# A 3x3 convolution with residual: first image in one load, residuals and stores two pairs at a time

## The chip, the cores and the metric

One core of one Trainium2 chip. Times are device microseconds of a whole execution; the lower the better. The traced span, from the kernel's first instruction to its last, is shorter than that time.

## The reference

```python
# x, residual: 16 x 64 x 64 x 64 float32; weight: 64 x 64 x 3 x 3
x_pad = np.pad(x, ((0, 0), (0, 0), (1, 1), (1, 1)))
for b, co, ci, kh, kw in all_of_them:
    output[b, co] += weight[co, ci, kh, kw] * x_pad[b, ci, kh:kh+64, kw:kw+64]
return output + residual
```

The inputs x and residual are 16.8 MB each, and so is the output. With 0.15 MB of weights, 50.48 MB cross the HBM interface, whatever the kernel does.

## The kernel before

Two images (a "pair", 2 MB) fill 128 partitions. ScalarE (ACT) casts an image to bf16, TensorE convolves it into PSUM, and VectorE (DVE) adds the residual in place in SBUF, from where it is stored. SyncE (SP) issues all the DMA but one. The parts that matter:

```python
sem = lambda name: tc.alloc_semaphore(name)
s_x = [sem(f"s_x{i}") for i in range(NXR)]
s_r = [sem(f"s_r{p}") for p in range(NPAIR)]          # one for each residual pair
# ... (20 in all)

for p in range(NPAIR):                                # SyncE
    if p >= NXR:
        nc.sync.wait_ge(s_half, 2 * (p - NXR) + 3)
    if p == 0:
        to_the_front(load_x(p, cols=slice(0, NPIX // 2)))   # before the opening barrier
        nc.sync.dma_start(out=wraw[:, :], in_=w_rows[:, :]).then_inc(s_w, 16)
    else:
        load_x(p)
    load_ro(p)
for p in range(NEARLY):                               # NEARLY = 6
    nc.sync.wait_ge(s_add, 2 * p + 3)
    store(p).then_inc(s_out, 16)
# ...
to_the_front(load_x(0, nc.scalar, slice(NPIX // 2, NPIX)))  # ACT: the image's other half
# ...
for n in range(B):                                    # VectorE
    p, im = divmod(n, 2)
    if im == 0:
        nc.vector.wait_ge(s_r[p], 16)
    # ... two adds; the first waits for the convolution
# ...
for p in range(NEARLY, NPAIR):                        # the last two stores
    store(p)
with tc.tile_critical(sync_engine=mybir.EngineType.Pool, no_gpsimd_drain=True):
    nc.gpsimd.wait_ge(s_out, 16 * NEARLY)             # GpSimd's closing wait
```

The last two stores carry no semaphore in the source. The built program gives each one of its own, and has GpSimd wait for the first of them and SyncE for both.

## Time and profile before

| | before |
|---|---|
| time | 122.9 us (122.8 to 123.06, 3 runs) |
| traced span | 121.17 us in a run of 123.0 us |
| TensorE, VectorE, ACT busy | 72%, 63%, 52% of the span |
| bytes at the full rate | 50.48 MB / 433 GB/s = 116.6 us |

Of the page of before: the span, the head of the chain that ended last, and the table of DMA issues (how many, KB each, us from issue to landing).

```profile
span 121.2 us, 736 instructions
PE 71%; DVEq 2%; DVE 2%; issue 0%
...
ro<-in_residual_dram SPq DMA_DIRECT2D x8, 2048.0 KB, 21.9
out_dram<-ro SPq DMA_DIRECT2D x8, 2048.0 KB, 28.2
xr<-in_x_dram SPq DMA_DIRECT2D x7, 2048.0 KB, 17.5
xr<-in_x_dram SPq DMA_DIRECT2D x1, 1024.0 KB, 7.0
xr<-in_x_dram ACTq DMA_DIRECT2D x1, 1024.0 KB, 7.6
wraw<-in_weight_dram SPq DMA_DIRECT2D x1, 144.0 KB, 6.9
```

The chain names PE, but 2 MB need only 4.86 us at the full rate, so a landing after 22 or 28 us means a queue of four or five transfers ahead of it: the engines are never without work. The prediction shows the slices that confirm it.

### The profile page before, as it was taken

How to read it: one execution, taken by the hardware profiler on the slowest of the kernel's cores; microseconds unless marked ns; L12 is line 12 of the kernel's file. 1: busy time of each engine (PE TensorE's matmuls, PEld its weight loads, DVE VectorE, ACT ScalarE, POOL GpSimd, SP SyncE). 2: the span in 40 equal slices, each digit the busy share in tenths (PEclk: the TensorE clock that was granted, in tenths of full speed). 3: DMA queues.
4: the chain of work that ended last, by engine and by line, in shares of the span. 5: the costliest groups of instructions: out<-in, count | busy, mean ns of one | idle time of the engine just before them, and what ended most of it. 6: DMA issues, size and time to landing. Idle time of an engine off the chain costs nothing.

```text
span 121.2 us, 736 instructions
## 1 busy us (share of the span) xinstructions
PE 87.7 (72%) x389; PEld 10.7 (9%) x105; DVE 76.0 (63%) x40; ACT 63.1 (52%) x37; POOL 2.4 (2%) x16
## 2 busy tenths in 40 slices
PE   0033499999999999999999999999999980000000
PEld 0021001101010101010101010101010100000000
DVE  0005300889898898989889898898989889300000
ACT  4049969938966984993993994896000000000000
POOL 5200000000000000000000000000000000000000
PEclk9999999999999999999999999999999999755555
DMA  6999999999999999999999999999999999999993
GB/s 168 427 444 433 433 433 433 433 427 433 433 427 427 433 433 427 427 433 427 433 433 433 433 433 422 433 389 433 433 433 433 422 433 433 433 433 433 427 433 151
DMA packets 3744, 50.48 MB, mean 417 GB/s; under 512 B 416, under 2 KB 544, under 8 KB 544
## 3 DMA queue, kind: packets, MB, share of 16 engines
q1 hardware_dynamic: 3600, 49.43, 96.3%
q10 hardware_dynamic: 144, 1.05, 2.0%
HBM read 33.70 MB, written 16.78 MB: 417 GB/s over the span
## 4 chain that ended last, share of the span: by engine, by line
PE 71%; DVEq 2%; DVE 2%; issue 0%
PE ps L86 53%; PE ps L85 17%; DVEq L129 2%; DVE ro L201 2%
## 5 line engine op out<-in xcount | busy, mean ns | idle before, releaser
L201 DVE TENSOR_TENSOR ro<-ps,ro 64x2048 f32<-64x2048 f32 x32 | 73.2, 2289 | 17.7 <-PE ps L86 17.2
L86 PE MATMUL ps<-xp,wl 128*128 128x504 bf16 (+1 forms) x288 | 80.0, 388 | 0.2
L173 ACT CAST xp<-xr 64x2048 bf16<-64x2048 f32 x16 | 30.3, 1896 | 19.3 <-DMA xr<-in_x_dram 17.1
L85 PE MATMUL ps<-xp,wl 128*128 128x504 bf16 (+1 forms) x92 | 35.8, 389 | 3.4 <-PEq L222 3.4
L177 ACT CAST xp<-xr 64x2048 bf16<-64x2048 f32 x16 | 30.4, 1897 | 0.4
L85 PEld LDWEIGHTS ps<-xp,wl 128*128 128x128 bf16 x96 | 9.5, 99 | 79.1 <-issue 79.1
L189 DVE CAST wl<-ps 32x192 bf16<-32x192 f32 x8 | 2.8, 348 | 10.4 <-PE ps L214 10.3
L214 PE MATMUL ps<-ident,wraw 128*32 128x128 f32 x9 | 2.1, 412 | 8.1 <-DMA wraw<-in_weight_dram 8.1
L214 PEld LDWEIGHTS ps<-ident,wraw 128*32 128x32 f32 x9 | 1.2, 137 | 8.6 <-issue 8.1
L173 ACT ACT_TABLE_LOAD x1 | 1.3, 1283 | 1.1 <-SPq L129 1.1
L182 ACT CAST wl<-ps 32x192 bf16<-32x192 f32 x4 | 1.2, 306 | 0.0
L160 POOL MEMSET xp<- 64x64 bf16 x4 | 0.6, 147 | 0.2
L159 POOL MEMSET xp<- 64x64 bf16 x4 | 0.6, 145 | 0.2
L148 POOL TENSOR_SCALAR_AFFINE_SELECT ident<-ident 128x128 f32<-128x128 f32 x1 | 0.3, 295 | 0.2 <-POOL ident L146 0.2
L162 POOL MEMSET wl<- 64x192 bf16 x1 | 0.3, 253 | 0.1
L161 POOL MEMSET wl<- 64x192 bf16 x1 | 0.3, 252 | 0.1
L146 POOL MEMSET ident<- 128x128 f32 x1 | 0.2, 205 | 0.7 <-SPq L129 0.7
L257 POOL MEMSET const-uint8-127<- 128x1 uint8 x1 | 0.1, 113 | 0.0
L257 POOL MEMSET const-bfloat16-1.0<- 128x1 bf16 x1 | 0.1, 112 | 0.0
L257 POOL MEMSET const-float32-1.0<- 128x1 f32 x1 | 0.1, 109 | 0.0
L257 POOL MEMSET const-float32-0.0<- 128x1 f32 x1 | 0.1, 104 | 0.2 <-issue 0.2
## 6 DMA issues: line engine op xcount, KB each, us to landing
ro<-in_residual_dram SPq DMA_DIRECT2D x8, 2048.0 KB, 21.9
out_dram<-ro SPq DMA_DIRECT2D x8, 2048.0 KB, 28.2
xr<-in_x_dram SPq DMA_DIRECT2D x7, 2048.0 KB, 17.5
xr<-in_x_dram SPq DMA_DIRECT2D x1, 1024.0 KB, 7.0
xr<-in_x_dram ACTq DMA_DIRECT2D x1, 1024.0 KB, 7.6
wraw<-in_weight_dram SPq DMA_DIRECT2D x1, 144.0 KB, 6.9
```

Of the source, the lines that this page charges most:

```text
L85: return e.matmul(out=out_, lhsT=lhsT, rhs=rhs, start=start, stop=stop, skip_group_check=True)
L86: return e.add_instruction(mybir.InstMatmult(name=nc.get_next_instruction_name(), engine=PE, ins=[e.lower_ap(rhs), e.lower_ap(lhsT)], outs ...
L129: with tc.tile_critical(no_gpsimd_drain=True):
L159: nc.gpsimd.memset(t[0:64, 0, :], 0.0).then_inc(s_id, 1)
L160: nc.gpsimd.memset(t[64:128, J, :], 0.0).then_inc(s_id, 1)
L173: i = nc.scalar.copy(out=t[64:128, 0:J, :], in_=x4[hp, :, 0, :])
L177: nc.scalar.copy(out=t[0:64, 1 : J + 1, :], in_=x4[hp, :, 1, :]).then_inc(s_pack, 1)
L182: i = nc.scalar.copy(**weight_block(h, *b))
L189: i = nc.vector.tensor_copy(**weight_block(h, *b))
L201: i = nc.vector.tensor_tensor(out=o4[hp, :, par, :], in0=psj[64 * par : 64 * par + 64, :, :], in1=o4[hp, :, par, :], op=ADD)
L214: i = nc.tensor.transpose(out=tp[0:32, t // 3, 128 * (t % 3) : 128 * (t % 3) + 128], in_=wraw3[:, :, t], identity=ident[:, :])
L257: nc = _bacc.Bacc("TRN2", target_bir_lowering=False, num_devices=1)
```

## The change

Its intent is economy around the bytes: fewer and larger transfers, fewer semaphores, one queue instead of two. The core of the diff (the renaming of s_wt into counts of s_id and the reshaping of `ro` into one tile are cut):

```diff
-    s_r = [sem(f"s_r{p}") for p in range(NPAIR)]
+    s_r = [sem(f"s_r{i}") for i in range(2)]
+    RES = (slice(0, 1), slice(1, 2), slice(2, 4), slice(4, 6), slice(6, 8))
...
+    def load_ro(i):
+        if i >= 2:
+            nc.sync.wait_ge(s_r[i % 2], 16 * (i // 2))
+        nc.sync.dma_start(out=ro[:, RES[i], :], in_=res_bc[:, RES[i], :]).then_inc(s_r[i % 2], 16)
...
-                to_the_front(load_x(p, cols=slice(0, NPIX // 2)))
+                to_the_front(load_x(p))
...
-            load_ro(p)
-        for p in range(NEARLY):
-            nc.sync.wait_ge(s_add, 2 * p + 3)
-            store(p).then_inc(s_out, 16)
+            if p in (0, 1, 3, 5, 7):
+                load_ro((p + 1) // 2)
+        for k in range(NSTORE - 1):
+            nc.sync.wait_ge(s_add, 4 * k + 5)
+            store(k).then_inc(s_out, 16)
...
-        to_the_front(load_x(0, nc.scalar, slice(NPIX // 2, NPIX)))
...
-            if im == 0:
-                nc.vector.wait_ge(s_r[p], 16)
+            if im == 0 and p in first:
+                i = first.index(p)
+                nc.vector.wait_ge(s_r[i % 2], 16 * (i // 2 + 1))
...
-    for p in range(NEARLY, NPAIR):
-        store(p)
+    store(NSTORE - 1)
```

Here `store(k)` moves pairs 2k and 2k+1, 4 MB.

More of the change, by code (lines that the diff above doesn't have):

```diff
@@ L37 @@
     NXP = 4
-    NEARLY = 6
-    res_bc = residual.rearrange("b c h w -> (b c) (h w)")
-    out_bc = out.rearrange("b c h w -> (b c) (h w)")
+    NZERO = 4 + 2 * NXP
+    NSTORE = NPAIR // 2
+    RES = (slice(0, 1), slice(1, 2), slice(2, 4), slice(4, 6), slice(6, 8))
+    res_bc = residual.rearrange("(p b) c h w -> (b c) p (h w)", b=2)
+    out_bc = out.rearrange("(p b) c h w -> (b c) p (h w)", b=2)
     x_bc = x.rearrange("b c h w -> (b c) (h w)")
@@ L48 @@
     ident = pool.tile([128, 128], FP32)
-    ro = [pool.tile([128, NPIX], FP32, name=f"ro{p}") for p in range(NPAIR)]
+    ro = pool.tile([128, NPAIR, NPIX], FP32)
     xr = [nc.alloc_sbuf_tensor(f"xr{i}", [128, NPIX], FP32) for i in range(NXR)]
@@ L59 @@
     s_x = [sem(f"s_x{i}") for i in range(NXR)]
-    s_r = [sem(f"s_r{p}") for p in range(NPAIR)]
+    s_r = [sem(f"s_r{i}") for i in range(2)]
     s_out = sem("s_out")
     s_id = sem("s_id")
-    s_wt = sem("s_wt")
     s_half = sem("s_half")
@@ L68, with load_x, store @@
     s_add = sem("s_add")
-    def load_x(p, engine=nc.sync, cols=slice(0, NPIX)):
-        return engine.dma_start(out=xr[p % NXR][:, cols], in_=x_bc[128 * p : 128 * p + 128, cols]).then_inc(
-            s_x[p % NXR], 16
-        )
-    def load_ro(p):
-        nc.sync.dma_start(out=ro[p][:, :], in_=res_bc[128 * p : 128 * p + 128, :]).then_inc(s_r[p], 16)
-    def store(p):
-        return nc.sync.dma_start(out=out_bc[128 * p : 128 * p + 128, :], in_=ro[p][:, :])
+    def load_x(p):
+        return nc.sync.dma_start(out=xr[p % NXR][:, :], in_=x_bc[128 * p : 128 * p + 128, :]).then_inc(s_x[p % NXR], 16)
+    def load_ro(i):
+        if i >= 2:
+            nc.sync.wait_ge(s_r[i % 2], 16 * (i // 2))
+        nc.sync.dma_start(out=ro[:, RES[i], :], in_=res_bc[:, RES[i], :]).then_inc(s_r[i % 2], 16)
+    def store(k):
+        pairs = slice(2 * k, 2 * k + 2)
+        return nc.sync.dma_start(out=out_bc[:, pairs, :], in_=ro[:, pairs, :])
     def matmul(out_, lhsT, rhs, start, stop, ldweights):
@@ L171 @@
             if im == 0:
-                nc.scalar.wait_ge(s_x[p % NXR], 16 * (p // NXR + 1 + (p % NXR == 0)))
+                nc.scalar.wait_ge(s_x[p % NXR], 16 * (p // NXR + 1))
             i = nc.scalar.copy(out=t[64:128, 0:J, :], in_=x4[hp, :, 0, :])
@@ L178 @@
             if n == 0:
-                nc.scalar.wait_ge(s_wt, 1)
+                nc.scalar.wait_ge(s_id, NZERO + 1)
                 for b in blocks[4:]:
@@ L182 @@
                         i = nc.scalar.copy(**weight_block(h, *b))
-                i.then_inc(s_wt, 1)
-        nc.vector.wait_ge(s_wt, 1)
+                i.then_inc(s_id, 1)
+        nc.vector.wait_ge(s_id, NZERO + 1)
         for k, b in enumerate(blocks[:4]):
@@ L191 @@
                     i.then_inc(s_bank, 2)
-        i.then_inc(s_wt, 1)
+        i.then_inc(s_id, 1)
+        first = [pairs.start for pairs in RES]
         for n in range(B):
@@ L195 @@
             hp = slice(64 * im, 64 * im + 64)
-            o4 = ro[p].rearrange("q (j two w) -> q j two w", two=2, w=W)
+            o4 = ro[:, p, :].rearrange("q (j two w) -> q j two w", two=2, w=W)
             psj = ps[n % 2].rearrange("q c j w -> q (c j) w")
-            if im == 0:
-                nc.vector.wait_ge(s_r[p], 16)
+            if im == 0 and p in first:
+                i = first.index(p)
+                nc.vector.wait_ge(s_r[i % 2], 16 * (i // 2 + 1))
             for par in range(2):
@@ L207 @@
                 i.then_inc(s_add if par == 0 or n == B - 1 else s_bank, 1)
-        nc.tensor.wait_ge(s_id, 4 + 2 * NXP)
+        nc.tensor.wait_ge(s_id, NZERO)
         nc.tensor.wait_ge(s_w, 16)
@@ L216 @@
             )
-        i.then_inc(s_wt, 1)
-        nc.tensor.wait_ge(s_wt, 3)
+        i.then_inc(s_id, 1)
+        nc.tensor.wait_ge(s_id, NZERO + 3)
         with nc.Fori(0, B // NXP, 1, engines=[PE]):
@@ L236 @@
                 m.then_inc(s_conv, 1)
-    for p in range(NEARLY, NPAIR):
-        store(p)
+    store(NSTORE - 1)
     with tc.tile_critical(sync_engine=mybir.EngineType.Pool, no_gpsimd_drain=True):
-        nc.gpsimd.wait_ge(s_out, 16 * NEARLY)
+        nc.gpsimd.wait_ge(s_out, 16 * (NSTORE - 1))
 _INS = ['x', 'weight', 'residual']
```

## The prediction

> **What bounds the kernel now.** I began with the chain of work that ended last, as one should, and here it misleads: it gives PE 71% of the span, but it ends at the last VectorE add (about 104 us) while the span is 121.2 us. So I went on to the slices and the DMA queues.
>
> ```profile
> PE   0033499999999999999999999999999980000000
> DMA  6999999999999999999999999999999999999993
> GB/s 168 427 444 433 433 433 433 433 427 433 433 427 427 433 433 427 427 433 427 433 433 433 433 433 422 433 389 433 433 433 433 422 433 433 433 433 433 427 433 151
> q1 hardware_dynamic: 3600, 49.43, 96.3%
> q10 hardware_dynamic: 144, 1.05, 2.0%
> HBM read 33.70 MB, written 16.78 MB: 417 GB/s over the span
> ```
>
> The 16 DMA engines are at 9 tenths or more in all slices but the first and the last, at 422 to 444 GB/s but for one dip to 389 near 80 us, where loads give way to stores. TensorE is done at slice 34 of 40. The kernel is bound by its bytes: 50.48 MB at 433 GB/s are 116.6 us. Only 4.6 us of the span are something else. Finer windows say where they are (columns: busy time of PE, PEld, DVE, ACT and POOL, then clock, DMA share, GB/s):
>
> ```profile
> 0.00:1.00 1.00, 0.00 (x0) 0.00 (x0) 0.00 (x0) 0.00 (x0) 0.22 (x4) 1.00 0.00 0
> 1.00:2.00 1.00, 0.00 (x0) 0.00 (x0) 0.00 (x0) 0.92 (x1) 0.59 (x3) 1.00 1.06 197
> 2.00:3.00 1.00, 0.00 (x0) 0.00 (x0) 0.00 (x0) 0.36 (x1) 0.73 (x6) 1.00 0.84 311
> 3.00:4.00 1.00, 0.00 (x0) 0.00 (x0) 0.00 (x0) 0.00 (x0) 0.78 (x5) 1.00 1.00 418
> 119.00:119.50 0.50, 0.00 (x0) 0.00 (x0) 0.00 (x0) 0.00 (x0) 0.00 (x0) 0.50 0.39 164
> 119.50:121.20 1.70, 0.00 (x0) 0.00 (x0) 0.00 (x0) 0.00 (x0) 0.00 (x0) 0.50 0.00 0
> ```
>
> Head: nothing flows for 1.0 us, and against 433 GB/s the next two microseconds lose (236 + 122) / 433 = 0.8 us. Tail: the last bytes are in by about 119.6 us; by the trace's semaphore records the last store is reported landed at 120.21 and the closing barriers run to 121.17. Together 1.0 + 0.8 + 1.6 = 3.4 us; the rest is the 80 us dip and the small weight packets. A change that adds and removes no byte can only win there, or lose by letting the queue run dry.
>
> It does not run dry before the end, because SyncE issues far ahead. The last two stores are issued once the last add is done:
>
> ```profile
> 104.42 0.96 SPq L79 DMA_DIRECT2D out_dram<-ro  x2
> SPq L268 <- DMA out_dram<-ro: 14.8, 2, 10.0
> ```
>
> At 104.42 us the store before them is still in the queue; it is reported at 110.50. SyncE then waits 14.8 us for data. The queue would empty only if the last issue slipped by more than about 4.5 us (110.5 minus 0.6 from last byte to report, minus 1.0 from issue to first packet, minus 104.4).
>
> **What the Trainium skill says.** "DMA: Bandwidth & Descriptors", section "Where 436 GB/s comes from", puts the ceiling of 16 engines at 435 GB/s. This trace agrees: 433 in most slices, so bigger transfers cannot raise the rate. The same page, "Issuing engines are not separate DMA queues": issuing from several engines saves only the sequencer's issue time. The trace agrees and is stronger: ACT's half of the first image was issued at 0.13 us, yet its first packet starts at 2.67 us, after 44 packets of SyncE's queue. The second queue bought nothing in the head. "Latency and other measured facts" there warns of tiles whose per-partition row pitch in HBM is 2 MiB or the like (164 GB/s). The changed transfers have a pitch of 16 KiB from partition to partition and 2 MiB only between a partition's two rows, so I do not expect it to apply; no run here shows it yet. "Why a DMA increments its semaphore by 16 and not by 1" warns of two transfers in flight on one semaphore; this is why the change has SyncE wait before it reuses one of the two residual semaphores.
>
> **The change part by part.**
>
> First image whole on SyncE. The 256 packets of 8 KB become 128 of 16 KB. In steady flow 8 KB takes 309 ns and 16 KB 611 ns, so 16 packets per engine at 309 (4.94 us) become 8 at 611 (4.89): -0.05 us. In the ramp the first packet of an engine took 0.5 to 1.3 us instead of 0.31. If that excess (about 0.6 us, then some 0.2 on the second packet) is a latency per packet or a fixed time, it stays whole; if it is lower speed until about 2.5 us in which a larger packet hides a bit more, some comes back. I take -0.15 us as an estimate. SyncE's first issue stays at time 0, and the barrier behind it, which now waits for no ACT issue (ACT joined it 0.1 us after SyncE), delays nothing that has bytes waiting. The image was complete at 7.75 us and the weights at 8.01 us; both stay within some tenths, as the same 2.24 MB pass first, and the compute chain has slack.
>
> Fewer transfers. 26 become 18. Each ends in one semaphore packet per engine, 9 ns in the trace: 8 x 9 ns = -0.07 us. The landings of 2 MB stores are 4.86 us apart, which their 8 packets of 608 ns fill already, so there is no gap between transfers to close.
>
> Residuals two pairs at a time. The order of loads becomes x2, x3, r2+r3, x4, x5, r4+r5, x6, x7, r6+r7. With the landings of before, x3 comes 4.9 us earlier (37.2 to 32.3) and r2 later, with r3, at 42.08 instead of 32.33. VectorE needs it for image 4:
>
> ```profile
> 42.46 4.61 DVE L201 TENSOR_TENSOR ro<-ps,ro 64x2048 f32<-64x2048 f32 x2 [0.58 <-PE ps L86]
> ```
>
> It is just in time, by 0.4 us. Pair 4 lands at 61.6 for an add at 63.2, pair 6 at 81.3 for an add at 84.0. So no wait arises, and one of 1 us would eat into the 4.5 us above without moving the end. SyncE's new waits (first use of a residual semaphore done) were met long before: r1 at 22.6 for an issue near 37, r2+r3 at 42 for one near 55.
>
> Stores two pairs at a time. The first waits for image 4's add (about 45 us, already over when SyncE gets there), the second for image 8's (65.5), the third for image 12's (86.3). The loads alone fill the engines to about 80.6 us, then each store of 4 MB adds 9.7: to 90, 100 and 109.7. Every issue is ahead of its deadline by 13 us or more; the last, at 104.4, by about the 4.5 us of before.
>
> The end. This is the part that the diff does not show. Before, the last two stores had two semaphores, and GpSimd's closing steps waited for the first alone. They ran under the last one: landed 115.36, GpSimd wakes 115.38, branch 115.47, semaphore 115.62, no-op 115.71. Now there is one last store, and the built program has GpSimd wait for it, while SyncE's final wait needs GpSimd's increment behind that no-op. So 115.71 - 115.36 = 0.35 us that lay under a transfer now follow it: +0.35 us. Fewer semaphores to clear: 200 ns for a range of 29 become, if proportional, 145 for 21: -0.05 us. Both kernels declare the same queues, so the 1.8 us between span and measured time (121.2 and 123.0 in the profiled run) should stay.
>
> Sum: -0.05 - 0.15 - 0.07 + 0.35 - 0.05 = +0.03 us, so 122.9.
>
> **Rivals.** (1) The head wins more: one queue of 16 KB packets reaches full rate at once. For it: between 1.0 and 2.67 us only SyncE's packets ran, 44 of 8 KB; the same 44 of 16 KB would be the full rate. Against: the engines were already occupied end to end by single slow packets. It would bring back those 0.8 us in place of my 0.15: 122.3. (2) The late residual stalls VectorE, then the PSUM banks, then the last issue. For it: only 0.4 us of margin at image 4. Against: a stall of even 2 us is under 4.5. It makes 0; with something unforeseen on top, +1. (3) Two rows 2 MiB apart per partition cost HBM rate. For it: the skill's figures for such strides. Against: at any moment the engines walk neighbouring rows as before. One per cent on the 29.4 MB that move so (residual pairs 2 to 7, 12.6 MB, and all stores, 16.8 MB: 68 us) would be +0.7 us, 123.6; a real collapse, several us. (4) The closing chain stays hidden: -0.35 us, 122.6.
>
> **Range and chances.** Head, tail and rate leave some +-0.6 us (the head up to -0.65 by rival 1, the tail -0.35 by rival 4, the rate +0.7 by rival 3, not all at once): 122.3 to 123.5. 2% is 2.46 us. To gain that, the span would have to be 118.7 us, which leaves 2.1 us beside the 116.6 of the bytes, less than the 1.0 before the first packet and the 1.6 after the last: 1%. To lose it needs rival 3 in force: 3%.
>
> **What would show it.** Right: DMA at 433 from slice 2 to 39; q10 gone; the last load-store order as above; VectorE's add of image 4 near 42.5 us; SyncE's last issue near 104; the last landing near 120.0; from landing to end 1.3 us instead of 0.96. Wrong: slices in the middle under 425 GB/s, a first slice near 250 GB/s, an add that waits for a residual by several us, or a DMA gap near 109 us.

## The result, and the profile after

The changed kernel takes 123.48 us (median, 123.28 to 123.73, 6 runs), before 122.9 (122.8 to 123.14, 6 runs); all were fast runs (none is over 1.5% above the fastest of its kernel). The ratio is 1.0044, 95% interval 1.003 to 1.0058. Ratios here are the mean time of one kernel's fast runs over that of the other's of the same rounds, so not quite the ratio of the medians quoted. The change makes the kernel slower by half a microsecond: "same" at 2%, but clear of noise, and at the edge of the predicted range.

The page of the changed kernel, profiled in its fastest run (123.28 us):

```profile
span 121.2 us, 729 instructions
DMA  7999999999999999999999999999999999999992
GB/s 173 427 416 433 433 433 432 433 433 432 433 432 432 433 432 433 433 432 432 422 427 433 432 433 427 432 422 432 432 433 432 432 427 433 432 432 433 432 432 108
q1 hardware_dynamic: 3488, 50.48, 98.1%
HBM read 33.70 MB, written 16.78 MB: 416 GB/s over the span
...
xr<-in_x_dram SPq DMA_DIRECT2D x8, 2048.0 KB, 15.2
out_dram<-ro SPq DMA_DIRECT2D x4, 4096.0 KB, 28.7
ro<-in_residual_dram SPq DMA_DIRECT2D x3, 4096.0 KB, 24.0
ro<-in_residual_dram SPq DMA_DIRECT2D x2, 2048.0 KB, 15.8
wraw<-in_weight_dram SPq DMA_DIRECT2D x1, 144.0 KB, 7.1
```

The second queue (q10) is gone, 26 transfers have become 18, and the rate is the same 432 to 433 in most slices. No slice in the middle is empty; two are at 422, under the 425 that the prediction named as a sign of being wrong, but before has two at 422 and one at 389 as well. The finer windows of the head and the tail (columns as in the prediction) answer to those of before:

```profile
0.00:1.00 1.00, 0.00 (x0) 0.00 (x0) 0.00 (x0) 0.03 (x1) 0.21 (x4) 1.00 0.00 0
1.00:2.00 1.00, 0.00 (x0) 0.00 (x0) 0.00 (x0) 1.00 (x1) 0.65 (x4) 1.00 1.27 229
2.00:3.00 1.00, 0.00 (x0) 0.00 (x0) 0.00 (x0) 0.25 (x1) 0.73 (x5) 1.00 0.86 295
3.00:4.00 1.00, 0.00 (x0) 0.00 (x0) 0.00 (x0) 0.00 (x0) 0.80 (x4) 1.00 0.90 377
119.00:119.50 0.50, 0.00 (x0) 0.00 (x0) 0.00 (x0) 0.00 (x0) 0.00 (x0) 0.50 0.02 0
```

From 1 to 4 us the three windows sum to 901 against 926 before: no faster start. (A packet counts in the window in which it starts.) Packet by packet, exactly 352 KB had been started before 2.67 us in both kernels, as 44 packets of 8 KB and as 22 of 16 KB (that they agree so exactly is chance: over all traces it is 336 to 400 KB, with no order by packet size), and the first image was complete at 7.75 us before and 7.73 after.

VectorE's add of image 4, SyncE's last issue, and SyncE's waits (us in total, times, longest):

```profile
42.31 4.61 DVE L205 TENSOR_TENSOR ro<-ps,ro 64x2048 f32<-64x2048 f32 x2 [0.58 <-PE ps L88]
...
104.27 0.37 SPq L81 DMA_DIRECT2D out_dram<-ro  x1
...
SPq L271 <- POOLq L244: 15.6, 1, 15.6
```

The add does not wait for its late residual, and the last issue is where it was. But SyncE's last wait has changed its releaser: before it was the store's DMA (the line in the prediction), now it is POOLq, GpSimd's queue. The instruction records say what happens there (us from the last store's landing):

| | before | after |
|---|---|---|
| last landing, us from the start | 120.21 | 119.91 |
| GpSimd wakes for its closing wait | 4.8 earlier, on the store before | +0.03 |
| GpSimd's branch, increment, no-op | done | +0.11, +0.26, +0.36 |
| SyncE passes its last wait | +0.04 | +0.40 |
| semaphores cleared, duration | 200 ns for 29 | 157 ns for 21 |
| end of the span | +0.96 | +1.31 |

So far +0.35 in the tail, and this trace has a last landing 0.3 us earlier, which leaves the spans equal (121.17 and 121.22). Yet the times of these two executions differ by 0.28 us (123.0 and 123.28). What lies outside the span was 1.83 us and is 2.06.

### The profile page after: what moved, and what is told of

The parts are those of the page before. It is cut to its first block, busy times and chain, and to the rows that moved or that the text cites. A ratio compares the mean times of both kernels' runs of the same rounds, so it can differ in the third digit from the quotient of the medians.

```text
span 121.2 us, 729 instructions
## 1 busy us (share of the span) xinstructions
PE 87.7 (72%) x393; PEld 10.7 (9%) x105; DVE 76.0 (63%) x40; ACT 63.1 (52%) x37; POOL 2.4 (2%) x16
## 4 chain that ended last, share of the span: by engine, by line
PE 71%; DVEq 2%; DVE 2%; issue 0%
PE ps L88 53%; PE ps L87 18%; DVEq L131 2%; DVE ro L205 2%
## 5 line engine op out<-in xcount | busy, mean ns | idle before, releaser
L205 DVE TENSOR_TENSOR ro<-ps,ro 64x2048 f32<-64x2048 f32 x32 | 73.2, 2289 | 17.4 <-PE ps L88 16.9
L88 PE MATMUL ps<-xp,wl 128*128 128x504 bf16 (+1 forms) x288 | 79.9, 387 | 0.0
L87 PE MATMUL ps<-xp,wl 128*128 128x504 bf16 (+1 forms) x96 | 37.2, 387 | 3.4 <-PEq L226 3.4
```

The source lines that it names most:

```text
L87: return e.matmul(out=out_, lhsT=lhsT, rhs=rhs, start=start, stop=stop, skip_group_check=True)
L88: return e.add_instruction(mybir.InstMatmult(name=nc.get_next_instruction_name(), engine=PE, ins=[e.lower_ap(rhs), e.lower_ap(lhsT)], outs ...
L205: i = nc.vector.tensor_tensor(out=o4[hp, :, par, :], in0=psj[64 * par : 64 * par + 64, :, :], in1=o4[hp, :, par, :], op=ADD)
```

## The experiments

Theory A: the closing chain behind the merged last store costs some 0.35 us, and nothing else in the trace does anything. Rival B: something outside the span grew as well. Each kernel was timed against before in the same rounds. All outputs are right. "Outside" is the time of the profiled run minus its span.

**The changed kernel again** (no edit).

> The changed kernel once more, so that the others are compared with it on one chip. Theory A (the closing chain of GpSimd now follows the last store, +0.34 us, and nothing else of the change moves the end by more than 0.1): ratio near 1.003, median near 123.3. Rival B (something outside the traced span also grew: the six runs were 2.08 to 2.15 us longer than their spans, the profiled run of before only 1.83): ratio near 1.0045, median near 123.5, and again about 0.25 us more outside the span than before.

123.54 us (123.39 to 123.89) against 123.05 of before: 1.0046 (1.0031 to 1.0061). From landing to end 1.31 us again, outside 2.07 us again. Rival B's numbers came. Its last landing was 120.01, so the 119.91 of the first trace was on the lucky side. One more thing was new:

```profile
42.31 2.28 DVE L205 TENSOR_TENSOR ro<-ps,ro 64x2048 f32<-64x2048 f32 x1 [1.20 <-DMA ro<-in_residual_dram]
```

Here the add of image 4 did wait for its residual. VectorE was idle for 1.2 us before it where 0.58 is usual, so the residual cost 0.6 us. It did so because TensorE had reached its faster pace 1.3 us earlier (17.4 instead of 18.7 us; see the end). The last landing did not move, as the 4.5 us in hand at the last issue said.

**The first image whole on SyncE, nothing else.**

```diff
# on the kernel before
-                to_the_front(load_x(p, cols=slice(0, NPIX // 2)))
+                to_the_front(load_x(p))
-        to_the_front(load_x(0, nc.scalar, slice(NPIX // 2, NPIX)))
-                nc.scalar.wait_ge(s_x[p % NXR], 16 * (p // NXR + 1 + (p % NXR == 0)))
+                nc.scalar.wait_ge(s_x[p % NXR], 16 * (p // NXR + 1))
```

> Before with the first image whole on SyncE's queue and no DMA from ACT; nothing else changed. Theory A: ratio 1.000 (within 0.001), the ramp as slow with 16 KB packets as with two queues of 8 KB, image complete near 7.7 us. Rival B, if ACT's missing DMA is what grew outside the span: +0.25 us, ratio 1.002, with the span near 121.2 and the time 2.1 us above it. Rival C (the single queue costs in the head): the span itself grows by 0.1 to 0.2 us.

122.82 us, 0.9985 (0.9971 to 0.9999). Outside 1.82 us, so ACT's missing DMA is not what grew. Image complete at 7.80 us: no gain in the head. The last landing, 120.01, was early; a repeat further down tests whether that is real.

**The last two stores merged, nothing else.**

```diff
# on the kernel before (ro made one tile, so that one transfer can take both pairs)
-    for p in range(NEARLY, NPAIR):
-        store(p)
+    nc.sync.dma_start(out=out_2[:, NEARLY:NPAIR, :], in_=ro_all[:, NEARLY:NPAIR, :])
```

> Before with its last two stores merged into one of 4 MB; all else as before. Theory A: the closing chain is exposed, +0.34 us: ratio 1.0028, from last landing to end 1.31 us instead of 0.97. Against A: ratio 1.000.

123.46 us, 1.0032 (1.0018 to 1.0046). Landing to end 1.34 us, outside 1.82. The wait that shows it, of this kernel:

```profile
SPq L269 <- POOLq L242: 17.1, 1, 17.1
```

**The changed kernel with its last store split.**

```diff
# on the changed kernel
-    store(NSTORE - 1)
+    for p in (NPAIR - 2, NPAIR - 1):
+        nc.sync.dma_start(out=out_bc[:, p, :], in_=ro[:, p, :])
```

> The changed kernel with its last store split again into pair 6 and pair 7, each with its own semaphore. Theory A: 0.34 us come back against the changed kernel on this chip; from last landing to end 0.93 us; ratio to before about 1.000, if all of the loss was the chain. Rival B: the chain comes back but 0.2 to 0.25 us stay, ratio 1.002.

123.0 us (122.97 to 123.01), 0.9996 (0.9982 to 1.0009). Landing to end 0.905 us, outside 2.06. SyncE waits for the stores again:

```profile
SPq L272 <- DMA out_dram<-ro: 14.9, 2, 10.1
```

These two settle the first half of theory A: merging the last stores exposes the chain, splitting them hides it. Both the changed and the split kernel clear 21 semaphores, so the chain's cost is 1.310 - 0.905 = 0.40 us. In time, split is 0.54 us under the changed kernel on the same chip; 0.40 is the chain and the rest lies within the scatter of the spans (120.9 in all five runs of the split kernel, 121.3 to 121.8 in those of the changed one). And 0.24 us outside the span stay, in a kernel with no exposed chain.

**What grew outside the span? First, the semaphores.**

```diff
# on the changed kernel
+    unused = [sem(f"s_unused{i}") for i in range(7)]
```

> The changed kernel with seven unused semaphores allocated, so that it has 20 again and all else as changed. The part of the time outside the traced span was 1.82 us in before, in the head-only and in the merged-last kernel, and 2.06 in the changed kernel (twice) and in the split-last one. Theory S (the number of semaphores sets that part): it falls to 1.82 us here. Theory P (the program's instructions or its other transfers set it): it stays at 2.06. Range clear 195 to 200 ns instead of 157 in both.

123.69 us, 1.0045 (1.0027 to 1.0064). Outside 2.07: theory S falls. The clear took 184 ns, below the 195 to 200 I expected, as its range was 28 semaphores and not 29.

**Paired residual loads alone.**

```diff
# on the kernel before (ro one tile)
-            load_ro(p)
+            if p < 2:
+                load_ro(p)
+            elif p % 2:
+                two = slice(p - 1, p + 1)
+                nc.sync.dma_start(out=ro_all[:, two, :], in_=res_2[:, two, :]).then_inc(s_r[p - 1], 16)
-            if im == 0:
+            if im == 0 and (p < 2 or p % 2 == 0):
                 nc.vector.wait_ge(s_r[p], 16)
```

> Before with residual pairs 2 to 7 loaded two at a time, nothing else. Theory: the span as before within 0.1 us, the add of image 4 near 42.4 us without a wait of over 0.3 us, and ratio 1.000. If theory P holds through the loads or VectorE's fewer waits (62 instructions become 59), the part outside the span is 2.06 us and the ratio 1.002; if not, 1.82.

123.51 us, 1.0033 (1.0013 to 1.0052). Outside 2.07: it is in this part. The expectation of no wait missed, as in the repeat above:

```profile
42.09 2.28 DVE L208 TENSOR_TENSOR ro_all<-ps,ro_all 64x2048 f32<-64x2048 f32 x1 [1.49 <-DMA ro_all<-in_residual_dram]
```

The last landing was 120.47 us, the latest of all traces. The delay was there before any store: its last load landed at 81.53 us, against 81.01 to 81.39 in all other traces, and from there to the last landing it took 38.95 us (the others 38.85 to 39.15). So it is scatter of the first 81 us, not the wait.

**Paired stores alone, the last two apart.**

```diff
# on the kernel before (ro one tile; GpSimd's closing wait counts three stores instead of six)
-        for p in range(NEARLY):
-            nc.sync.wait_ge(s_add, 2 * p + 3)
-            store(p).then_inc(s_out, 16)
+        for p in range(0, NEARLY, 2):
+            nc.sync.wait_ge(s_add, 2 * p + 5)
+            nc.sync.dma_start(out=out_2[:, p : p + 2, :], in_=ro_all[:, p : p + 2, :]).then_inc(s_out, 16)
```

> Before with the first six stores made three of 4 MB, the last two as before. Theory: ratio 1.000 and a last landing within 0.1 us of before; no gap in the DMA rate at 109 us. If theory P holds through the stores (SyncE's 46 instructions become 43), the part outside the span is 2.06 us; if not, 1.82.

123.1 us, 1.0001 (0.9982 to 1.002). Outside 1.83, last landing 120.27. Two rows 2 MiB apart per partition cost nothing, and fewer transfers win nothing.

**VectorE's program or the paired transfers?** The paired loads come with three waits fewer on VectorE: its program has 59 instructions instead of 62 (counted in the built program). Next, one kernel with the transfers of before and 59 instructions, and kernels with the paired transfers and other counts.

```diff
# on the kernel before: same transfers, two of them on one semaphore
     def load_ro(p):
+        to = p if p < 2 else p - p % 2
-        nc.sync.dma_start(...).then_inc(s_r[p], 16)
+        nc.sync.dma_start(...).then_inc(s_r[to], 16)
-            if im == 0:
-                nc.vector.wait_ge(s_r[p], 16)
+            if im == 0 and (p < 2 or p % 2 == 0):
+                nc.vector.wait_ge(s_r[p], 16 if p < 2 else 32)
```

> Before with all its transfers one pair each and in the same order, but VectorE waits once for residual pairs 2+3, 4+5, 6+7 (one semaphore each), three waits fewer: 59 instructions. Theory V: 2.06 us outside the span, ratio 1.002. Theory R: 1.82 us, ratio 1.000. The span stays within 0.1 us of before in both; pair 3 lands at about 42.1 and image 4's add begins at about 42.4.

123.37 us, 1.0032 (1.0013 to 1.0051). Outside 2.06, with every transfer as before: theory R falls, and theory V's number came. (Its four runs spread from 123.18 to 123.77, spans 121.1 to 121.7, hence the ratio above 1.002.)

```diff
# on the changed kernel: a wait for a load that landed long before
+            if im == 0 and p == 3:
+                nc.vector.wait_ge(s_x[0], 16)
```

> The changed kernel with one more wait on VectorE (for a load that landed long before), so VectorE has 60 instructions where before has 62, the changed kernel 59. The unused semaphores left the part outside the span at 2.07 us, and paired residual loads alone made it 2.07, paired stores alone did not. Theory V (VectorE's number of instructions sets that part): in proportion it would be 1.98 us, as a step 2.06 or 1.82. Theory R (the paired residual transfers themselves set it): 2.06. The wait itself costs VectorE under 0.1 us, off the path.

123.58 us, 1.0039 (1.0024 to 1.0055). Outside 2.215: neither the proportion (1.98) nor one of the two steps. One instruction more made it worse.

```diff
# on the split kernel: three such waits
+            if im == 0 and p in (3, 5, 7):
+                nc.vector.wait_ge(s_x[(p - 3) // 2], 16)
```

> The changed kernel with the last store split and three more met waits on VectorE (62 instructions again). Theory V: 1.82 us outside the span and from landing to end 0.91 us, so 0.24 below the split-last kernel and 0.55 to 0.6 below the changed one: median near 122.75, ratio to before 0.998. Theory R: 2.06 us and median near 123.0.

122.97 us, 0.999 (0.9977 to 1.0003). Outside 1.825, landing to end 0.906: both losses are gone, with all transfers of the change but the last store in place. The time missed the expected 122.75 because its span was 121.0 to 121.3 on this chip, not 120.9.

> The head-only kernel again, beside the one that keeps most of the change, to see whether its 0.9985 (0.9971 to 0.9999) repeats. Expected if it is real: ratio 0.9985, median near 122.85, last landing near 120.0 where before had 120.2. If it was luck of one chip: 1.000.

123.01 us, 0.9998 (0.9984 to 1.0012); last landing 120.20. The 0.9985 did not repeat.

Last, 61 instructions (the split kernel with two such waits):

> The changed kernel with the last store split and two more met waits on VectorE: 61 instructions. The part outside the span so far by VectorE's instructions: 59: 2.06 us, 60: 2.215, 62: 1.82. If it rises by 0.155 us an instruction and falls back once in between, 61 gives 1.67 (fall between 60 and 61) and this would be the fastest kernel, median near 122.8 and ratio to before near 0.9975; or 2.37 (fall between 61 and 62), median near 123.5. If it has no such order, neither.

123.38 us, 1.0014 (0.9994 to 1.0033). Outside 2.23. Neither number came; there is no rise by 0.155 an instruction. The table gathers what is outside the span. The range is over all runs, whose spans are given to 0.1 us:

| VectorE's instructions | kernels | outside, profiled run | all runs |
|---|---|---|---|
| 62 | before; head only (twice); merged last; paired stores; split with three waits | 1.82 to 1.83 | 1.77 to 1.88 |
| 61 | split with two waits | 2.23 | 2.21 to 2.29 |
| 60 | changed with one wait | 2.215 | 2.20 to 2.27 |
| 59 | changed (twice); split last; unused semaphores; paired loads; three fewer | 2.06 to 2.07 | 2.02 to 2.15 |

The five kernels with 62 and the five with 59 have nothing else in common, of what was looked at, that would divide them: both groups hold kernels with and without ACT's DMA, with split and merged last stores, with 20 and with 13 semaphores. The waits added or taken are met at once or nearly so, and VectorE is not on the path that sets the end. Shortening another engine's program did nothing: SyncE's went from 46 to 43 with the paired stores, ACT's from 57 to 56 in the head-only kernel, and both stayed at 1.82 to 1.83. But VectorE's length was changed by waits alone, so its length and its number of waits are not told apart.

## Why the prediction was right, and where it was wrong

It said 122.9 in a range of 122.3 to 123.5, within 2%. The time was 123.48, inside the range, but two terms of its sum were wrong and they nearly used up the range. That it still fell inside is partly luck: the range was drawn for the head, the tail and the rate, and 0.24 us came from a term that was put at 0.

| step | predicted | measured |
|---|---|---|
| engines bound by bytes, no gap, rate kept | yes | yes: 432 to 433 GB/s in most slices, no gap near 109 us |
| larger first packets win part of the ramp | -0.15 | none: 352 KB by 2.67 us in both, image at 7.75 and 7.73 |
| fewer semaphore packets, no 8 KB packets | -0.12 | not to be told from the scatter of the last landing |
| GpSimd's closing chain exposed | +0.35 | +0.40 (1.310 - 0.905) |
| shorter clear | -0.05 | -0.04 (200 to 157 ns) |
| outside the span | 0 | +0.24 (1.83 to 2.06) |
| sum | +0.03 | +0.60; by the ratios of two sets of rounds +0.54 and +0.57 |

The closing chain, read from the built program and the records of before, was the right mechanism and nearly the right size. It is the larger half of the loss.

The first step that failed is that "the 1.8 us between span and measured time" should stay. The reason given was that both kernels declare the same queues. The experiments put 0.24 us there, and it goes with the length of VectorE's program: 59 instructions against 62, whatever else the kernel does. The prediction does not mention that VectorE loses three waits. What stays open is the mechanism. The length is not a cost per instruction (59, 60, 61 and 62 give 2.06, 2.215, 2.23 and 1.82). The Trainium skill ("Runtime: NRT & Kernel Launch", section "The ~15µs preamble/postamble breakdown") lists what runs around a kernel, barriers and resets of 51 semaphores on each engine. The trace agrees that they are there: the resets end 1.33 us after the span in every kernel, and the last barrier's updates end 1.94 to 1.95 us after it in all traces but one. They end so with 59 and 60 instructions too, so the 0.24 and 0.39 us of these kernels show in no recorded update, before the span or after it. (The 1.82 us of the kernels with 62 instructions are less than these 1.94, so the measured time does not run from the span's start to the last update. Where it begins and ends is not recorded.)

The exception is the kernel with 61 instructions, and there the loss can be seen. Its last barrier ends 2.34 us after the span: the last four of the barrier's nine updates come 0.50 us after the five before them, and in every other trace 0.10 us after. These 0.40 us are all that this kernel has more outside the span. Which engine was late, and why, the records do not say. A late fetch of instructions is an obvious candidate that was not tested; the packets that the traces mark as instruction fetches all start before the span or in its first 0.2 us.

The second is the ramp. The estimate of -0.15 rested on one of the cases that the prediction named: lower speed until about 2.5 us, in which a larger packet "hides a bit more". Lower speed is what the traces show: an engine's first packet took 0.5 to 1.3 us for 8 KB and 1.05 to 1.99 us for 16 KB, so the excess over the steady 0.31 and 0.61 us grew with the packet. But the larger packet hid nothing: the bytes by 2.67 us were the same, and so was the landing of the first image. Rival 1, which rested on the same hope, falls with it.

Rival 2 (the late residual stalls VectorE) was half right. The margin of 0.4 us was read from one trace, and in four others VectorE was idle for 1.2 to 1.5 us before the add, 0.6 to 0.9 us more than usual. Nothing came of it, because of the 4.5 us in hand at the last issue. Rival 3 (two rows 2 MiB apart) did not occur. Rival 4 (the chain stays hidden) is refuted by the merged and the split kernel.

Of the versions tried none is faster than before in a way that repeats: the head-only kernel's 0.9985 became 0.9998, and the split last store with three extra waits is at 0.999 (0.9977 to 1.0003).

## What to carry to other kernels

When the DMA engines are full from end to end and the rate stays, as here, only what lies before the first and after the last byte can change the time, so look there first: at which instructions wait for the last transfer. Merging the last transfers makes everything that waited for the earlier one wait for the whole; leave a last transfer of its own, here 2 MB, that nothing but the end waits for. And compare measured times with spans before explaining a half per cent by the trace, since it may not be in the trace at all.

## What the Trainium skill lacked or had wrong

- "Runtime: NRT & Kernel Launch" gives no figure for a time outside the kernel that depends on the length of one engine's program. Here it was 1.82, 2.23, 2.215 and 2.06 us for 62, 61, 60 and 59 instructions on VectorE. With 61 the last barrier ended at 2.34 us after the span instead of 1.94; with 60 and 59 no recorded update moved. Why is open.
- "DMA: Bandwidth & Descriptors" says under "Latency and other measured facts" that the first byte comes after about 600 ns. The trace agrees if one counts from the end of the issue (first packet at 1.01 us, issue ended at 0.39), but the page lacks the slow start after it: 352 KB in the first 1.67 us, half of what 433 GB/s give (336 to 400 KB over all traces), for 8 KB and 16 KB packets alike.
- The same page, "Queues, rings and completion order", has each engine go round-robin between its queues. In before, the second queue's transfer, issued at 0.13 us, got its first packet only at 2.67 us, after 44 packets of the first queue on 16 engines; in the four other kernels with that queue it was 2.35 to 2.65 us. No run shows why.
- Its warning of HBM row pitches does not reach two rows 2 MiB apart in one partition, if the partitions lie 16 KiB apart: 4 MB transfers ran at 432 to 433 GB/s.
- "TensorE: Matmul & The Clock Gate", section "Part 1: The HAM clock gate (the "warmup" mystery)", has TensorE run at half pace at first. It gives two measures of how the end of this varies: +-500 ns, and 6, 11 or 14 slow matmuls of one and the same kernel. The traces fit the second and not the first: blocks of four 512-column matmuls went from 1.71 to 0.87 us between 2.9 us (16.5 us) and 5.8 us (19.6 us) after the first convolution began, which is after 7 to 14 matmuls. This decided whether VectorE waited for a residual: in the nine kernels whose residual for image 4 lands at about 42 us, it did not where the change came at 18.6 us or later, and it did where it came at 18.1 us or before.
